# A hybrid encoder step on one Trainium2 core: the next block's activation differences move to mid-block and through DRAM, and a block's last and first steps move later

## The chip, the core and the metric

The kernel runs on one core of a Trainium2 chip. A core has five engines that each work through their own queue in order: TensorE (PE in the profile, with PEld for loading weights into it), VectorE (DVE), ScalarE (ACT), GpSimd (POOL) and SyncE (SP). SP here issues nearly all transfers between DRAM and the on-chip memory. The metric is the time of one execution in microseconds. The median of three runs of the kernel before is 2237.77 us (2236.51 to 2239.1).

## The reference, cut to what matters

The program is one layer of a streaming encoder for 2048 prompt frames and 64 further frames, 1024 features each, in float32.

```
q, k, v, u, vm = project(x @ w_in)
mix = concat(rmsnorm(window_attention(q, k, v)), rmsnorm(u * (w_s vm + b))) @ w_out
h   = layernorm(alpha * x + mix)
gu  = h @ w_gate_up                       # 1024 -> 2 * 2816
f   = (silu(gu[:, :2816]) * gu[:, 2816:]) @ w_down
y   = layernorm(alpha * h + f)
```

The change concerns the last three lines alone, the feed-forward part, which takes the second two thirds of the time.

## The kernel before

**Blocks and chunks.** The 2112 frames are cut into four blocks (512, 512, 512 and 576 frames; 17 tiles of 128 frames, the last with 64). For each block the hidden width 2816 is worked through in 22 chunks of 128 (NFF). A float32 product is made of three fast ones: each operand is split into a high part (a cast by ScalarE, L106) and a low part (a subtraction, L107, by VectorE or by POOL), and hi x hi, hi x lo and lo x hi are added in PSUM.

**Seven products for eight.** h @ w_gate_up is a two by two block product (frames in two halves by gate and up, features in two halves), and it is computed with the Strassen-Winograd scheme: seven products, numbered 1 to 7 (P1 to P7 here), for eight. For that the kernel needs sums and differences of the weights (`sums`, `form`; kept in DRAM after block 0 as wf_d and loaded from there later) and differences of the activations: with b11, b12, b21, b22 for the quarters of h (by feature half and frame half), P5 takes b12 - b11, P6 takes b22 - (b12 - b11), P7 takes b22 - b12 and P4 takes b21 - (b22 - (b12 - b11)); P1, P2 and P3 take b11, b21 and b22. Each operand lies, split, in a tile of its own (hf1 to hf7), with one buffer each: the next block's can be written only when the product of the old block's last chunk has read it.

**The order.** `order` lists the products of a block: P1, 5, 6, 2, 7 of the first chunk, then for each further chunk P1 of it, P4 and P3 of the chunk before, and P5, 6, 2, 7; at the end P4 and P3 of the last: 154 products. A product is 12 matmuls (L788 to L790) into one of three PSUM banks of its chunk (accA, accB, accC). P1, P6, P7 and P4 add up in accA, and between them ScalarE copies the bank out (`keep`, L794), before the next of them may go on writing there. `make` prepares the weights of the product five places ahead (LOOK), in one of seven buffers.

**Everything else is hung on positions of that list** (`at`, `todo`): after the product at a position, the functions registered there are issued, and each engine gets them in that order. Per two chunks these are: four loads and splits of w_down (`load_d`, `split_d`), and one down unit per tile and half (`down`: 6 matmuls, then L1129 adds the result to y). A block's last down units, with the tiles' last steps (`finish_steps`: two bn_stats, the aggregate and a pow on POOL (L86); norm, which first makes a small factor with shift_of on VectorE (L1151) and then scales on ScalarE (L1166); gain on VectorE, L1170; shift on POOL, L1174, and the store) and the load of the next block's y tile (`new_y`, L1136) fall among the first products of the next block.

**The differences before.** `prep_steps(b + 1)` loads b11 and b12 some 20 positions ahead of the boundary, subtracts on POOL (L691), loads b22 and b21 at the boundary and goes on subtracting there in a shared tile, with the splits into hf (`put`) between the subtractions.

## Time and profile before

| | us |
|---|---|
| median of three runs | 2237.77 |
| the profiled execution | 2239.35 |
| its span, first to last instruction | 2237.6 |
| TensorE busy in it | 2122.9 (95%) |
| VectorE, ScalarE, POOL busy | 1488.9, 955.5, 602.7 |
| mean granted TensorE clock | 0.974 of full speed |

In the profile a row of instructions has its start, its duration, engine, source line, operation, what it writes and reads, and in brackets how long the engine stood idle before it and what ended that. A row of the table of stretches has a stretch, its length, busy time and number of instructions of each engine, the granted share of TensorE's clock, the busy share of the DMA engines and what they moved.

### The profile page before, as it was taken

The numbers are of one execution on the slowest core, as the hardware profiler recorded it, in microseconds if no ns is written. First come the engines' busy times: TensorE is split into PE (matmuls) and PEld (weight loads), VectorE is DVE, ScalarE is ACT, GpSimd is POOL, SyncE is SP. The second block draws the span as 40 slices with busy tenths as digits, with TensorE's granted clock in tenths as the row PEclk, the third lists the DMA queues.
The fourth block names the chain that finished last, engine by engine and source line by source line (L and its number), as shares of the span: only waits on it lengthen the run. The fifth ranks groups of instructions, "written<-read, shape, count | busy, mean of one in ns | idle before, by whom it ended". The sixth has DMA issues, their size and how long they took to land.

```text
span 2237.6 us, 35543 instructions
## 1 busy us (share of the span) xinstructions
PE 2122.9 (95%) x13219; PEld 1901.1 (85%) x13219; DVE 1488.9 (67%) x2919; ACT 955.5 (43%) x2255; POOL 602.7 (27%) x542
## 2 busy tenths in 40 slices
PE   8999999989998999998799999979999979999996
PEld 6888888867886899997799999879999969999994
DVE  6877777787896788887755555764555674444446
ACT  6666666654443444444333333433333332323332
POOL 0222222231224545555311112331111331111112
PEclk9999999999999999999899999989999989999998
DMA  5111111145646767676566667666666656555551
GB/s 194 38 39 39 39 38 47 35 137 177 222 164 223 258 229 250 222 244 240 202 235 228 211 216 241 217 230 225 218 209 231 244 182 231 193 193 186 191 180 57
DMA packets 161132, 400.23 MB, mean 179 GB/s; under 512 B 19744, under 2 KB 45600, under 8 KB 160960
## 3 DMA queue, kind: packets, MB, share of 16 engines
q1 hardware_dynamic: 140432, 379.29, 49.7%
q10 hardware_dynamic: 20352, 18.35, 2.4%
q8 instruction: 104, 1.70, 0.3%
q14 instruction: 68, 0.56, 0.1%
q0 software_dynamic: 176, 0.33, 0.0%
HBM read 316.84 MB, written 81.07 MB: 178 GB/s over the span
## 4 chain that ended last, share of the span: by engine, by line
PE 47%; DVE 4%; ACT 1%; issue 1%; DVEq 0%; ACTq 0%
PE pd L152 6%; PE pd L153 6%; PE accA L788 6%; PE pd L154 6%; PE accA L790 6%; PE accA L789 6%; PE accC L788 3%; PE accC L790 3%; PE accC L789 3%; PE accB L789 1%; PE accB L790 1%; PE accB L788 1%; DVE y L1170 0%; ACT wd L106 0%; DVE hf L107 0%
## 5 line engine op out<-in xcount | busy, mean ns | idle before, releaser
L107 POOL TENSOR_TENSOR wf<-guraw,wf 128x512 fp32r<-128x512 f32 x173 | 241.1, 1394 | 821.5 <-ACT wf L106 798.1
L788 PE MATMUL accA<-hf,wf 128*128 128x256 f32 (+1 forms) x1408 | 410.5, 292 | 44.6 <-ACT a L794 39.9
L790 PE MATMUL accA<-hf,wf 128*128 128x256 f32 (+1 forms) x1408 | 407.3, 289 | 0.8 <-POOL wf L107 0.6
L789 PE MATMUL accA<-hf,wf 128*128 128x256 f32 (+1 forms) x1408 | 405.0, 288 | 0.0
L1129 DVE TENSOR_TENSOR y<-pd,y 128x512 f32<-128x512 f32 (+1 forms) x364 | 249.8, 686 | 185.2 <-PE pd L154 176.6
L788 PEld LDWEIGHTS accA<-hf,wf 128*128 128x128 f32 x1408 | 269.1, 191 | 57.6 <-ACT a L794 44.2
L152 PE MATMUL pd<-wd,ff 128*128 128x512 f32 (+1 forms) x728 | 291.1, 400 | 9.8 <-ACT wd L106 9.8
L153 PE MATMUL pd<-wd,ff 128*128 128x512 f32 (+1 forms) x728 | 289.9, 398 | 0.5 <-DVE wd L107 0.5
L154 PE MATMUL pd<-wd,ff 128*128 128x512 f32 (+1 forms) x728 | 287.6, 395 | 0.0
L789 PEld LDWEIGHTS accA<-hf,wf 128*128 128x128 f32 x1408 | 270.5, 192 | 8.5
L790 PEld LDWEIGHTS accA<-hf,wf 128*128 128x128 f32 x1408 | 269.1, 191 | 1.4 <-POOL wf L107 0.8
L107 DVE TENSOR_TENSOR wd<-draw,wd 128x512 fp32r<-128x512 f32 x176 | 171.7, 979 | 71.7 <-ACT wd L106 66.3
L794 ACT COPY a<-accA 128x256 f32<-128x256 f32 (+1 forms) x264 | 99.6, 377 | 262.6 <-PE accA L790 260.4
L788 PE MATMUL accC<-hf,wf 128*128 128x256 f32 (+1 forms) x704 | 203.6, 289 | 0.6 <-ACT wf L106 0.6
L790 PE MATMUL accC<-hf,wf 128*128 128x256 f32 (+1 forms) x704 | 202.7, 288 | 0.3 <-DVE wf L107 0.3
L789 PE MATMUL accC<-hf,wf 128*128 128x256 f32 (+1 forms) x704 | 201.6, 286 | 0.0
L106 ACT CAST ff<-a 128x256 fp32r<-128x256 f32 (+1 forms) x176 | 72.7, 413 | 289.0 <-DVE a L801 289.0
L154 PEld LDWEIGHTS pd<-wd,ff 128*128 128x128 f32 (+1 forms) x728 | 135.9, 187 | 35.1
L106 ACT CAST wf<-guraw 128x512 fp32r<-128x512 f32 x264 | 163.0, 618 | 5.5 <-PE po L154 2.9
L152 PEld LDWEIGHTS pd<-wd,ff 128*128 128x128 f32 (+1 forms) x728 | 136.5, 187 | 29.7 <-ACT wd L106 11.5
L153 PEld LDWEIGHTS pd<-wd,ff 128*128 128x128 f32 (+1 forms) x728 | 136.6, 188 | 18.3 <-DVE wd L107 2.0
L107 DVE TENSOR_TENSOR ff<-a,ff 128x256 fp32r<-128x256 f32 (+1 forms) x176 | 91.2, 518 | 84.4 <-ACT ff L106 84.4
(282 smaller groups left out, 4833.5 us busy)
## 6 DMA issues: line engine op xcount, KB each, us to landing
wf<-wf_d SPq DMA_DIRECT2D x264, 512.0 KB, 4.5
guraw<-in_w_gate_up_dram SPq DMA_DIRECT2D x110, 512.0 KB, 4.9
wf_d<-wf SPq DMA_DIRECT2D x88, 512.0 KB, 5.6
draw<-in_w_down_dram SPq DMA_DIRECT2D x176, 256.0 KB, 4.4
guraw<-in_w_gate_up_dram SPq DMA_DIRECT2D x66, 256.0 KB, 2.9
x<-in_xT_prompt_dram SPq DMA_DIRECT2D x32, 256.0 KB, 3.1
catx<-cat_d SPq DMA_DIRECT2D x16, 512.0 KB, 3.6
catx<-in_x_prompt_dram SPq DMA_DIRECT2D x16, 512.0 KB, 4.6
```

Source lines behind the costliest of these rows:

```text
L106: nc.scalar.copy(hi, src)
L107: (on or nc.vector).tensor_tensor(out=lo, in0=src, in1=hi.bitcast(F32), op=ALU.subtract)
L152: nc.tensor.matmul(out, ah, bh, start=(i == 0), stop=False)
L153: nc.tensor.matmul(out, ah, bl, start=False, stop=False)
L154: nc.tensor.matmul(out, al, bh, start=False, stop=(i == n - 1))
L788: nc.tensor.matmul(ps, wh, hh, start=(new and k == 0), stop=False, skip_group_check=not new)
L789: nc.tensor.matmul(ps, wh, hl, start=False, stop=False, skip_group_check=not new)
L790: nc.tensor.matmul(ps, wl, hh, start=False, stop=(k == 3), skip_group_check=not new)
L794: nc.scalar.copy(part[i, key][:, :n], ps)
L1129: nc.vector.tensor_tensor(out=y, in0=pd[:m], in1=y, op=ALU.add)
```

## The change

The differences of the next block are made some 100 to 64 products ahead of its first one, with loads of their own, and stored in DRAM (hs_d). Near the boundary each operand then needs one load per half (`fetch`) and its split (`put`). The last down units of a block move six positions later, the last steps of its tiles five to nine; shift_of becomes a step of its own, two positions ahead of the norm. The first down units of the next block move some three to five positions later and go by half, not by tile, and the loads and splits of w_down around are placed anew. The diff, cut to that:

```diff
+    hs_d = [{p: dram.tile([P, 4, TB[b] // 2], F32, name=f"hs_d{b}_{p}") for p in (4, 5, 6, 7)} for b in range(NB)]
...
+    def later_steps(b):
...
+        def sub(out, x, y, kk, prod):
+            if (out, kk) not in t:
+                t[out, kk] = piece("hsum")
+            nc.gpsimd.tensor_tensor(out=t[out, kk], in0=t[x, kk], in1=t[y, kk], op=ALU.subtract)
+            nc.sync.dma_start(out=hs_d[b][prod][:, 2 * kk:2 * kk + 2], in_=t[out, kk])
+
+        def fetch(prod, kk, tag):
+            t[prod, kk] = piece(tag)
+            where = {1: (0, 0), 2: (1, 0), 3: (1, 1)}.get(prod)
+            src = hs_d[b][prod][:, 2 * kk:2 * kk + 2] if where is None else (
+                h_d[b][:, 4 * where[0] + 2 * kk:4 * where[0] + 2 * kk + 2, where[1] * n:(where[1] + 1) * n])
+            nc.sync.dma_start(out=t[prod, kk], in_=src)
...
+        for kk in range(2):
+            q = -100 + 24 * kk
+            yield q, lambda kk=kk: load("b11", kk, 0, 0)
+            yield q, lambda kk=kk: load("b12", kk, 0, 1)
+            yield q + 1, lambda kk=kk: load("b22", kk, 1, 1)
+            yield q + 1, lambda kk=kk: load("b21", kk, 1, 0)
+            yield q + 6, lambda kk=kk: sub("t1", "b12", "b11", kk, 5)
+            yield q + 8, lambda kk=kk: sub("t2", "b22", "t1", kk, 6)
+            yield q + 10, lambda kk=kk: sub("b12", "b22", "b12", kk, 7)
+            yield q + 12, lambda kk=kk: sub("b21", "b21", "t2", kk, 4)
+        for prod, tag, fetch_at, put_at in ((1, "hraw", -24, -8), (5, "hraw", -22, -5), (6, "hsum", -20, -4), (2, "hraw", -6, -2),
+                                            (7, "hraw", -3, 0), (4, "hsum", -1, 2), (3, "hraw", 1, 4)):
+            for kk in range(2):
+                yield fetch_at + kk, lambda prod=prod, kk=kk, tag=tag: fetch(prod, kk, tag)
+                yield put_at + kk, lambda prod=prod, kk=kk: put(prod, kk)
...
         def norm():
-            shift_of(s_, m)
             nc.scalar.activation(y_t[t][:m], y_t[t][:m], AF.Identity, scale=s_["rs"][:m, 0:1], bias=s_["rs"][:m, 1:2])
...
-        return [lambda: stats(s_, (z(0), z(1)), m, 0), lambda: (stats(s_, (z(0), z(1)), m, 1), moments(s_, m)), norm, gain, shift]
+        return [lambda: stats(s_, (z(0), z(1)), m, 0), lambda: (stats(s_, (z(0), z(1)), m, 1), moments(s_, m)),
+                lambda: shift_of(s_, m), norm, gain, shift]
...
-            if c in (0, NFF // 2 - 1) or last and c == NFF // 2 - 2:
+            if c == 0 and b:
+                d_load, d_split = (-5, 1, -3, 2), (0, 6, 3, 7)
+            elif c == 1 and b:
+                d_load, d_split = (-8, -1, -4, 1), (-3, 7, 2, 8) if last else (-3, 5, 1, 6)
+            elif c == NFF // 2 - 1 and not last:
+                d_load, d_split = (0, 2, 1, 6), (5, 7, 6, 9)
+            elif last and c == NFF // 2 - 2:
...
-                    units_.sort(key=lambda e: e[1])
-                    where = (3, 4, 6, 7, 9, 10, 12, 13, 14, 15)
...
+                    where = (6, 10, 12, 14, 15, 16, 17, 18, 19, 20) if last else (6, 10, 12, 14, 15, 16, 17, 18)
...
-                        at(p0 + 4 + 2 * k + h, lambda b=b, c=c, t=t, h=h: down(b, c, t, h))
+                        at(p0 + 10 + 2 * k + h, lambda b=b, c=c, t=t, h=h: down(b, c, t, h))
                     steps = finish_steps(t)
-                    for q, f in zip((6, 7, 10, 11, 12), steps):
+                    for q, f in zip((11, 12, 14, 16, 17, 19), steps):
                         at(p0 + 2 * k + q, f)
-                    at(p0 + 2 * k + 14, lambda t=new.pop(0): new_y(t)) if new else None
+                    at(p0 + 2 * k + 21, lambda t=new.pop(0): new_y(t)) if new else None
         if not last:
-            for pos, f in prep_steps(b + 1):
-                at(first + NO - 1 + pos, f)
+            for pos, f in later_steps(b + 1):
+                at(first + NO + pos, f)
```

On ScalarE, at the boundary from block 1 to block 2, these were the rows up to the first copy of the new block's accA (a0<-accA); hf6 and hf7 are the split operands of P6 and P7, and hsum holds a difference that POOL makes:

```order
L106 CAST hf6_15650<-hsum_15283 128x512
L106 CAST hf7_15617<-hraw_15208 128x512
L823 ACTIVATE a1_15550<-a1_15550 128x256
L106 CAST ff_15635<-a1_15550 128x256
L106 CAST hf6_15650<-hsum_15316 128x512
L106 CAST wf_15689<-guraw_15511 128x512
L794 COPY a0_15705<-accA_15692 128x256
```

Now, up to the same copy; hf2 is the operand of P2, b21 as loaded:

```order
L877 ACTIVATE a1_15633<-a1_15633 128x256
L108 CAST ff_15714<-a1_15633 128x256
L108 CAST hf2_15726<-hraw_15646 128x512
L108 CAST wf_15764<-guraw_15599 128x512
L848 COPY a0_15780<-accA_15767 128x256
L108 CAST hf7_15784<-hraw_15697 128x512
```

The splits of differences ahead of the copy have gone, and those of P7 stand behind it.

On POOL, at the same boundary, the last steps of block 1's four tiles stood so; yrs is the pow, y the shift, wf the low part of weights:

```order
L86 TENSOR_TENSOR yrs_15866<-rs_e_15867,neg_half_201 128x1
L107 TENSOR_TENSOR wf_15880<-guraw_15740,wf_15880 128x512
L86 TENSOR_TENSOR yrs_15929<-rs_e_15930,neg_half_201 128x1
L86 TENSOR_TENSOR yrs_15997<-rs_e_15998,neg_half_201 128x1
L1174 TENSOR_TENSOR y_11929<-y_11929,ln2b_7948 128x512 x2
L107 TENSOR_TENSOR wf_16040<-guraw_15740,wf_16040 128x512
L86 TENSOR_TENSOR yrs_16063<-rs_e_16064,neg_half_201 128x1
L1174 TENSOR_TENSOR y_12256<-y_12256,ln2b_7948 128x512 x2
L107 TENSOR_TENSOR wf_16095<-guraw_15943,wf_16095 128x512
L1174 TENSOR_TENSOR y_12304<-y_12304,ln2b_7948 128x512 x2
```

Now:

```order
L88 TENSOR_TENSOR yrs_16042<-rs_e_16043,neg_half_217 128x1
L109 TENSOR_TENSOR wf_16056<-guraw_15813,wf_16056 128x512
L88 TENSOR_TENSOR yrs_16106<-rs_e_16107,neg_half_217 128x1
L109 TENSOR_TENSOR wf_16118<-guraw_15967,wf_16118 128x512
L88 TENSOR_TENSOR yrs_16172<-rs_e_16173,neg_half_217 128x1
L88 TENSOR_TENSOR yrs_16242<-rs_e_16243,neg_half_217 128x1
L1227 TENSOR_TENSOR y_11964<-y_11964,ln2b_7964 128x512 x2
L109 TENSOR_TENSOR wf_16271<-guraw_15967,wf_16271 128x512
L1227 TENSOR_TENSOR y_12442<-y_12442,ln2b_7964 128x512 x2
L109 TENSOR_TENSOR wf_16329<-guraw_16188,wf_16329 128x512
L1227 TENSOR_TENSOR y_12502<-y_12502,ln2b_7964 128x512 x2
```

All four pow operations stand ahead of the first shift now; the fourth stood behind it and behind a weight form.

On SP, at the same boundary, the issues from the weights of P7 of the new block's first chunk (wf_d0_7) to those of P5 of its second (wf_d1_5) were (guraw is w_gate_up, y the next tile):

```order
L754 DMA wf_15657<-wf_d0_7_111 128x1024
L686 DMA hraw_15686<-h_d2_89 128x2x256
L754 DMA wf_15738<-wf_d0_3_108 128x1024
L735 DMA guraw_15740<-in_w_gate_up_dram 128x1024
L735 DMA guraw_15742<-in_w_gate_up_dram 128x512
L1136 DMA y_15758<-hy_d8_99 128x1024
L754 DMA wf_15762<-wf_d1_5_113 128x1024
```

Now, from the second row after the weights of P7 on (draw is w_down):

```order
L741 DMA hsum_15762<-hs_d2_4_116 128x512
L1166 DMA draw_15782<-in_w_down_dram 128x512
L741 DMA hsum_15787<-hs_d2_4_116 128x512
L1166 DMA draw_15805<-in_w_down_dram 128x512
L741 DMA hraw_15809<-h_d2_89 128x2x256
L808 DMA wf_15811<-wf_d0_3_124 128x1024
L789 DMA guraw_15813<-in_w_gate_up_dram 128x1024
L789 DMA guraw_15815<-in_w_gate_up_dram 128x512
L1190 DMA y_15831<-hy_d8_99 128x1024
L741 DMA hraw_15836<-h_d2_89 128x2x256
L808 DMA wf_15838<-wf_d1_5_129 128x1024
```

The loads of the differences for P4 (hsum) and of h for P3 (hraw) and two of w_down have come between; the last hraw is the fifth issue counted from the weights of P3.

## Rows read from the trace of the kernel before

**Rows 1.** The page, busy time of each engine (share of the span, instructions).

```profile
PE 2122.9 (95%) x13219; PEld 1901.1 (85%) x13219; DVE 1488.9 (67%) x2919; ACT 955.5 (43%) x2255; POOL 602.7 (27%) x542
```

**Rows 2.** TensorE: a product, a down unit, first P6 matmul of two blocks.

```profile
1014.36 0.28 PE L788 MATMUL accA<-hf,wf 128*128 128x256 f32 x1
...
1015.80 0.40 PE L152 MATMUL pd<-wd,ff 128*128 128x512 f32 x1
...
1017.20 0.28 PE L788 MATMUL accC<-hf,wf 128*128 128x256 f32 x1
...
1059.54 0.58 PE L788 MATMUL accA<-hf,wf 128*128 128x256 f32 x1 [6.96 <-ACT a L794]
...
1425.11 0.39 PE L788 MATMUL accA<-hf,wf 128*128 128x256 f32 x1 [0.74 <-ACT a L794]
```

**Rows 3.** Stretches: PE, PEld, DVE, ACT, POOL busy (count), clock, DMA, GB/s.

```profile
1000.00:1020.00 20.00, 20.00 (x141) 18.64 (x140) 15.82 (x23) 8.26 (x18) 11.88 (x10) 1.00 0.85 303
1040.00:1060.00 20.00, 12.31 (x82) 11.09 (x81) 11.62 (x19) 7.41 (x17) 10.80 (x8) 0.86 0.77 264
1060.00:1080.00 20.00, 18.80 (x103) 16.95 (x103) 14.63 (x23) 7.45 (x17) 5.58 (x5) 0.79 0.48 160
1100.00:1120.00 20.00, 9.33 (x46) 7.87 (x47) 11.76 (x17) 7.82 (x14) 9.77 (x7) 0.66 0.61 230
1420.00:1440.00 20.00, 16.84 (x101) 14.86 (x101) 15.59 (x24) 8.75 (x19) 5.90 (x4) 0.91 0.62 216
1460.00:1480.00 20.00, 8.80 (x50) 7.16 (x50) 14.88 (x22) 6.59 (x12) 10.09 (x8) 0.69 0.60 203
1780.00:1800.00 20.00, 15.70 (x94) 14.28 (x93) 17.06 (x22) 10.64 (x22) 10.64 (x7) 0.91 0.57 189
1820.00:1840.00 20.00, 14.43 (x95) 12.75 (x93) 15.21 (x26) 7.51 (x13) 10.27 (x9) 0.91 0.51 183
1840.00:1860.00 20.00, 14.87 (x82) 13.88 (x83) 10.92 (x18) 6.67 (x13) 7.88 (x6) 0.75 0.78 266
```

**Rows 4.** Waits of TensorE, 700 to 2200 us: total, times, longest.

```profile
PE accA L788 <- ACT a L794: 39.9, 13, 8.0
```

**Rows 5.** Instructions of POOL and ScalarE at boundary 0/1.

```profile
1047.68 1.29 POOL L691 TENSOR_TENSOR hsum<-hraw,hsum 128x512 f32<-128x512 f32 x1 [6.07 <-DMA hraw<-h_d]
...
1058.09 0.61 ACT L106 CAST hf<-hsum 128x512 fp32r<-128x512 f32 x1
```

**Rows 6.** Instructions of ScalarE and VectorE in the second place of boundary 0/1.

```profile
1101.12 1.24 ACT L1166 ACTIVATE y<-y,yrs 128x1024 f32<-128x1024 f32 x1 [2.62 <-DVE yrs L1151]
...
1108.78 1.21 DVE L1151 SCALAR_TENSOR_TENSOR yrs<-ymv,yrs 128x1 f32<-128x1 f32 x1
...
1110.03 1.24 ACT L1166 ACTIVATE y<-y,yrs 128x1024 f32<-128x1024 f32 x1 [3.98 <-DVE yrs L1151]
```

**Rows 7.** Gains on VectorE; POOL beside the second; a shift on POOL.

```profile
1087.66 1.28 DVE L1170 TENSOR_TENSOR y<-y,ln2g 128x512 f32<-128x512 f32 x2
...
1094.31 2.38 DVE L1170 TENSOR_TENSOR y<-y,ln2g 128x512 f32<-128x512 f32 x2
...
1094.32 1.83 POOL L107 TENSOR_TENSOR wf<-guraw,wf 128x512 fp32r<-128x512 f32 x1 [1.20 <-issue]
...
1106.67 3.31 POOL L1174 TENSOR_TENSOR y<-y,ln2b 128x512 f32<-128x512 f32 x2 [1.86 <-DVE y L1170]
```

**Rows 8.** A stretch; issues (count, size, us to landing); one issue on SP.

```profile
1480.00:1490.00 10.00, 10.00 (x64) 9.16 (x64) 4.05 (x9) 3.44 (x9) 4.51 (x4) 0.94 0.98 368
...
wf<-wf_d SPq DMA_DIRECT2D x264, 512.0 KB, 4.5
...
hraw<-h_d SPq DMA_DIRECT2D x24, 256.0 KB, 5.1
...
1410.26 0.41 SPq L754 DMA_DIRECT2D wf<-wf_d  x1
```

**Rows 9.** A subtraction on POOL in block 0.

```profile
1014.61 1.30 POOL L691 TENSOR_TENSOR hsum<-hraw 128x512 f32<-128x512 f32 x1
```

More of the change, by code (lines that the diff above doesn't have):

```diff
@@ L710, in prep_steps, with piece, load, put @@
                 yield at_ + kk, lambda fn=fn, a=a: fn(*a)
+    def later_steps(b):
+        t = {}
+        n = TB[b] // 2
+        def piece(tag):
+            return f1.tile([P, 2 * NHX], F32, name=tag, tag=tag, bufs={"hraw": 4, "hsum": 2}[tag])[:, :2 * n].rearrange(
+                "p (k t) -> p k t", k=2)
+        def load(key, kk, kh, sh):
+            t[key, kk] = piece("hraw")
+            k0 = 4 * kh + 2 * kk
+            nc.sync.dma_start(out=t[key, kk], in_=h_d[b][:, k0:k0 + 2, sh * n:(sh + 1) * n])
+        def sub(out, x, y, kk, prod):
[9 more added lines that the diff above has]
+            nc.sync.dma_start(out=t[prod, kk], in_=src)
+        def put(prod, kk):
+            if kk == 0:
+                forms[b, prod] = f1.tile([P, 8 * NHX], F32R, name=f"hf{prod}", tag=f"hf{prod}", bufs=1)[:, :8 * n].rearrange(
+                    "p (s k t) -> p s k t", s=2, k=4)
+            o = forms[b, prod][:, :, 2 * kk:2 * kk + 2]
+            split(o[:, 0], o[:, 1], t.pop((prod, kk)))
+        for kk in range(2):
[13 more added lines that the diff above has]
+                yield put_at + kk, lambda prod=prod, kk=kk: put(prod, kk)
@@ L1283, in hybrid_step @@
                 where = (2, 3, 4, 5, 7, 8, 9, 10, 12, 13) if last else (2, 4, 5, 7, 9, 10, 12, 13)
-                units_ = [(h, t) for h in range(2) for t in TILES[b]]
                 if c == 0 and b:
-                    units_.sort(key=lambda e: e[1])
-                    where = (3, 4, 6, 7, 9, 10, 12, 13, 14, 15)
-                for k, (h, t) in enumerate(units_):
+                    where = (6, 10, 12, 14, 15, 16, 17, 18, 19, 20) if last else (6, 10, 12, 14, 15, 16, 17, 18)
+                elif c == 1 and last:
+                    where = (3, 4, 5, 6, 7, 9, 10, 11, 12, 13)
+                for k, (h, t) in enumerate((h, t) for h in range(2) for t in TILES[b]):
                     at(p0 + where[k], lambda b=b, c=c, t=t, h=h: down(b, c, t, h))
```

## The prediction

> **What bounds the kernel now.** I read the engines' busy times first. TensorE is busy for 95% of the span [rows 1], so only time in which it stands still or runs at half clock can be won. Its own work in the second half is fixed: 12 matmuls of a product take 1.44 us (1014.36 to 1015.80), the 6 of a down unit 1.40 us [rows 2]. A block of 22 chunks has 154 products and 88 down units, so 154 x 1.44 + 88 x 1.40 = 345.0 us of work. The same matmul (first of the product P6 of a block's first chunk) starts at 1059.54 in block 1 and at 1425.11 in block 2 [rows 2]: 365.6 us. So about 20.6 us per block are lost, and the question is where.
>
> The table of stretches answers it [rows 3]. In mid-block TensorE is busy 20.00 of 20.00 us at full clock. Around a boundary it isn't. I count a stretch's loss as its idle time plus (1 - granted clock) x its busy time:
> - Boundary 0/1: 7.69 + 1.72, 1.20 + 3.95, and later 10.67 + 3.17: 28.4 us.
> - Boundary 1/2: 3.16 + 1.52, later 11.20 + 2.73: 18.6 us (the block period said 20.6).
> - Boundary 2/3: 4.30 + 1.41, later 5.57 + 1.30 and 5.13 + 3.72: 21.4 us.
>
> The sum is 68.4 us, in two places: 25.0 us when the new block begins and 43.4 us some 35 to 45 us later. In the second place idle time is 32.6 and the clock 10.9, so each idle microsecond drags about a third of one behind it; in the first the two are 16.4 and 8.6.
>
> The list of waits then says for what TensorE waits: almost only for ScalarE's copy of a PSUM bank, accA (L794), 39.9 us in 13 waits [rows 4]. ScalarE is far from full, so something stands before the copy in its queue.
> - First place: a split of the differences does. It waits for POOL's subtractions, and the first of four in a row starts only when h_d data have landed, at 1047.68; ScalarE splits the last hsum at 1058.09, then comes the copy, and TensorE starts at 1059.54 [rows 5, 2].
> - Second place: the norm (L1166) of a finished tile. It starts at 1101.12 after 2.62 us of waiting and at 1110.03 after 3.98, each time for the tiny shift_of (L1151) on VectorE, which took 1.21 us instead of its usual fraction at 1108.78 [rows 6]. Two norms are 8.91 us apart: ScalarE and VectorE wait for each other in turn, and the copy and the splits of w_down are queued behind.
>
> **The change part by part.** Slots are counted from a block's first product (slot 0).
>
> Differences in mid-block. Per boundary 8 subtractions of 1.29 us (10.3 us of POOL) leave the boundary. Instead of 8 transfers there are 30: 8 loads and 8 stores in mid-block, 14 loads at the boundary, all issued by SP; SP waits at each store for POOL, and behind it stand weight loads that have five products of lead. In block 0, where POOL is busiest, two of the subtractions of before ran from 1014.61 on [rows 9], and TensorE was busy 20.00 of 20.00 with POOL at 11.88 and VectorE at 15.82 [rows 3]. Four within 7 products and 4 units (15.7 us) make POOL 9.3 + 5.2 = 14.5 of 15.7: it still fits. Bounds: 0, and 10.3 if none is covered, in block 0 alone. I take 1 us, near the row.
>
> First steps. The 14 splits of 0.61 us on ScalarE [rows 5] stay as many; none waits for POOL any longer, and in the new order the copy that TensorE needs has one split and one weight cast ahead of it. What is late next is the last load, the second half of h for P3. It is the fifth issue from a weight load that needs the buffer of product 0; at 0.41 us an issue [rows 8] it goes out 2.1 us after slot 1 begins. It lands 5.1 us later [rows 8] and takes some 1.3 us to split, 0.61 on ScalarE [rows 5] and as much on VectorE: 8.5 us. P3's second half is needed after six products and a half, 9.4 us. That is in time with 0.9 us of room. Taken away entirely, the first place costs 0; if it stays as in the two later boundaries, 4.7 or 5.7. I take 3 per boundary, half of it and a little; for the first boundary too, since its extra 9 us came from the subtractions' late start.
>
> Last steps. The down units of the last chunk pair move from slots 3 to 10 to slots 9 to 16, so slots 0 to 8 are products alone. The four steps of a tile become five, and shift_of stands two slots ahead of the norm instead of in front of it. On POOL all four small pow operations now stand ahead of the first shift, where one stood behind two tensor operations. So a norm finds its scale ready, the turn-taking loses its cause, and new_y, a load that waits for the output's store, is still two slots later. The cover gets thinner though: the gains fall on slots 16 to 22, of which five have no down unit. A gain took 1.28 us alone and 2.38 with a POOL operation beside it [rows 7]. Three of the four will meet POOL's shifts (3.31 us at 1106.67 [rows 7]): 3 x 1.10 = 3.3 us, with a third for the clock 4.4; I take 5. Bounds: 1 (all covered) and the 13.8 to 15.7 of now.
>
> On this POOL and VectorE stretch each other in the rows. The Trainium skill (SBUF — State Buffer, Who interferes with whom) goes further: a VectorE instruction with two inputs in SBUF and a GpSimd instruction that reads SBUF hold the shared port for a whole instruction, and the other blocks. The trace agrees with a lengthening of 1.10 for a pair of gains, but not of one whole POOL operation for each.
>
> The new times of the w_down loads and splits, the order of the units by half, and block 0's first chunk pair, which now has the ordinary offsets, I cost at nothing: each split still stands slots ahead of its unit, beside products.
>
> Sum: 3 x 3 + 3 x 5 + 1 = 25 us stay of 68.4: 43.4 us are won. The profiled execution took 2239.35 us (span 2237.6), so 2196.0; the median of the three runs is 1.6 lower, hence **2194 us**.
>
> **The rivals.**
> - Nearly all goes: 2 us stay per boundary. For it: nothing in mid-block loses anything. Against: slots 0 to 8 have no cover. 2237.8 - 62.4 = 2175 us.
> - Transfers. SP's 23 issues from the load for slot -1 to that for slot 9 carry 8.65 MB (7 x 512, 2 x 768, 3 x 256, 8 x 256, 512 KB), where before 19 carried 7.60 MB. TensorE has 11 x 1.44 + 4 x 1.40 = 21.4 us for them: 404 GB/s, above the 368 of the best stretch [rows 8]. At 368 they end 2 us late, which the weights' lead hides (six products, 8.6 us, less 4.5 to land: 4.1). At the 266 of 1840 to 1860 [rows 3] they take 32.5 us: 11.1 late, 7.0 idle, 9.3 with the clock. That is 6.3 more than taken, three times: 2213 us.
> - Every gain operation waits out a POOL operation: 8 x 1.29 = 10.3, with the clock 13.7 instead of 5 per boundary: 2220 us. For it: the 2.38; against: the 1.28 of its neighbour. It is what the rule of the Trainium skill named above would give.
> - Slower: the turn-taking stays, through the gains and the mults that still alternate between ScalarE and VectorE. Four tiles at 8.91 us are 35.6 us, now in slots 15 to 24, where TensorE has 20.0 us of work: 15.6 idle, 20.8 with the clock, and 3 for the first place: 71.4 + 1, that is 2242 us. It decides from 8.7 us a tile on. Against it: its link, the norm behind shift_of, is the one that is cut.
> - The change doesn't do what it says: the norm then waits for statistics instead and the splits for the loads: 2235 us.
>
> **How the numbers follow.** Forecast (2184 to 2206) 0.43; nearly all 0.18; transfers 0.11; port 0.10; slower 0.11; no effect 0.05; something between 0.02. A measurement of this kernel can tell 0.2%, some 4.5 us. Faster: 0.43 + 0.18 + 0.11 + 0.10 + 0.02 = 0.84; same 0.05; slower 0.11. The range reaches from the case in which nearly all goes to just above the port's: 2175 to 2228.
>
> **What would show it.** Right: the same matmul in blocks 1 and 2 about 353 us apart (345 + 8); waits of accA for L794's successor under 12 us in place of 39.9; norms under 6 us apart; no POOL subtraction within 40 us of a boundary and no idle TensorE beside those in mid-block. Transfers: waits of TensorE for weights or for hf in slots 2 to 9. Port: gains of 2.4 us and more, four times per boundary. Wrong altogether: norms still 9 us apart, or half clock for over 10 us after a boundary.

## The result, and the profile after

The kernel after takes 2204.64 us (median of four runs, 2202.89 to 2205.52) against 2238.43 of the kernel before in the same runs: a ratio of 0.9849 [0.9832, 0.9867]. 33.8 us were won where 43.4 were forecast; 2204.64 lies inside the range. The profiled execution took 2202.89 us with a span of 2201.1.

In the kernel after, the matmuls of a product are L842 to L844, the copy of accA is L848, the splits are L108 (ScalarE) and L109, a down unit's matmuls L154 to L156 and its add L1183, shift_of L1205, norm L1219, gain L1223, shift L1227, the loads of the operands L741. First the page's line of busy times, and the first P6 matmul of a first chunk in blocks 1 and 2:

```profile
PE 2113.0 (96%) x13219; PEld 1895.4 (86%) x13219; DVE 1483.8 (67%) x2919; ACT 955.9 (43%) x2255; POOL 612.0 (28%) x542
```

```profile
1048.82 0.28 PE L842 MATMUL accA<-hf,wf 128*128 128x256 f32 x1
...
1405.40 0.28 PE L842 MATMUL accA<-hf,wf 128*128 128x256 f32 x1
```

The instruction counts are those of [rows 1]: the work has not changed. TensorE is busy 9.9 us less; its mean granted clock is 0.984, before 0.974. The two matmuls are 356.6 us apart, where they were 365.6 [rows 2] and 353 were forecast. The table of stretches (columns as in [rows 3]) shows what is left:

```profile
900.00:920.00 20.00, 20.00 (x135) 18.37 (x134) 17.50 (x24) 9.17 (x21) 15.26 (x11) 1.00 0.86 302
...
1040.00:1060.00 20.00, 18.06 (x135) 17.12 (x136) 14.17 (x25) 11.65 (x26) 4.43 (x3) 1.00 1.03 402
...
1060.00:1080.00 20.00, 20.00 (x134) 18.36 (x133) 13.58 (x29) 7.25 (x17) 4.91 (x5) 1.00 0.66 227
...
1080.00:1100.00 20.00, 18.55 (x131) 16.96 (x130) 18.36 (x28) 7.42 (x13) 12.17 (x10) 1.00 0.66 218
1100.00:1120.00 20.00, 15.13 (x92) 14.29 (x93) 12.05 (x23) 8.32 (x18) 6.68 (x5) 0.83 0.95 337
1400.00:1420.00 20.00, 17.44 (x125) 16.77 (x125) 13.78 (x23) 10.96 (x24) 4.36 (x3) 0.91 0.84 294
1440.00:1460.00 20.00, 17.44 (x127) 16.09 (x125) 18.29 (x28) 6.36 (x13) 13.28 (x10) 1.00 0.62 206
1460.00:1480.00 20.00, 16.23 (x97) 15.16 (x98) 11.05 (x21) 8.60 (x18) 5.62 (x5) 0.83 0.99 359
1760.00:1780.00 20.00, 19.26 (x136) 18.55 (x135) 14.68 (x25) 13.13 (x27) 4.43 (x3) 1.00 0.87 311
1800.00:1820.00 20.00, 16.28 (x111) 15.14 (x109) 16.79 (x24) 7.77 (x14) 12.91 (x10) 0.98 0.65 201
1820.00:1840.00 20.00, 18.56 (x106) 17.27 (x107) 10.65 (x19) 6.96 (x16) 5.42 (x4) 0.85 0.98 367
```

Counted as in the prediction, the first place now costs 1.9, 4.1 and 0.7 us, and the second 8.9, 9.1 and 8.3. The first row lies in block 0, where the subtractions now are: POOL is busy for 15.26 of 20 us, and TensorE loses nothing. In the second place VectorE is busy for 18.4 and 18.3 of the 20 us ahead of the longest wait (16.5 between 1080 and 1100 us before). In the 20 us with the wait it is busy for 12.05, about as before (11.76 [rows 3]). The list of TensorE's waits, 700 to 2200 us:

```profile
PE accA L842 <- ACT a L848: 22.7, 11, 5.8
...
PE accC L842 <- ACT hf L108: 3.6, 2, 2.2
```

The wait for the copy fell from 39.9 [rows 4] to 22.7. The second line is new. It is the first place: P3 (in accC) waits for the second half of its operand. Of boundary 0/1 these are the first matmul of P5 (slot 1), the two issues of w_gate_up on SP, the load's issue, the split on ScalarE that waited for it, and TensorE:

```profile
1047.38 0.28 PE L842 MATMUL accC<-hf,wf 128*128 128x256 f32 x1
...
1048.73 2.11 SPq L789 DMA_DIRECT2D guraw<-in_w_gate_up_dram  x2
...
1051.37 0.42 SPq L741 DMA_DIRECT2D hraw<-h_d  x1
...
1057.65 0.62 ACT L108 CAST hf<-hraw 128x512 fp32r<-128x512 f32 x1 [1.59 <-DMA hraw<-h_d]
...
1058.32 0.38 PE L842 MATMUL accC<-hf,wf 128*128 128x256 f32 x1 [1.43 <-ACT hf L108]
...
1415.70 0.38 PE L842 MATMUL accC<-hf,wf 128*128 128x256 f32 x1 [2.21 <-ACT hf L108]
```

The load went out 4.0 us after slot 1 began, and the split could start 6.28 us after the issue. The five issues didn't follow each other at 0.41 us: SP waited 2.1 us before the two loads of w_gate_up, and 2.0 at boundary 1/2, for a low part of weights on VectorE; there too the load went out 4.0 us after slot 1 began. The last row is the same matmul at boundary 1/2. Now the second place of boundary 0/1, the instructions of VectorE, POOL, ScalarE and TensorE in order of time:

```profile
1083.62 1.28 DVE L1223 TENSOR_TENSOR y<-y,ln2g 128x512 f32<-128x512 f32 x2
...
1086.34 0.15 DVE L1205 SCALAR_TENSOR_TENSOR yrs<-ymv,yrs 128x1 f32<-128x1 f32 x1
...
1088.19 2.99 POOL L1227 TENSOR_TENSOR y<-y,ln2b 128x512 f32<-128x512 f32 x2
...
1088.55 1.46 DVE L109 TENSOR_TENSOR wd<-draw,wd 128x512 fp32r<-128x512 f32 x1 [1.02 <-ACT wd L108]
...
1090.27 3.15 DVE L1223 TENSOR_TENSOR y<-y,ln2g 128x512 f32<-128x512 f32 x2
...
1091.13 1.74 POOL L109 TENSOR_TENSOR wf<-guraw,wf 128x512 fp32r<-128x512 f32 x1
1092.83 3.00 POOL L1227 TENSOR_TENSOR y<-y,ln2b 128x512 f32<-128x512 f32 x2
...
1093.34 1.25 DVE L1205 SCALAR_TENSOR_TENSOR yrs<-ymv,yrs 128x1 f32<-128x1 f32 x1
...
1095.39 0.72 DVE L109 TENSOR_TENSOR ff<-a,ff 128x256 fp32r<-128x256 f32 x1 [0.47 <-ACT ff L108]
1096.04 2.38 DVE L1223 TENSOR_TENSOR y<-y,ln2g 128x512 f32<-128x512 f32 x2
...
1097.83 3.40 POOL L1227 TENSOR_TENSOR y<-y,ln2b 128x512 f32<-128x512 f32 x2
...
1098.34 1.76 DVE L109 TENSOR_TENSOR wd<-draw,wd 128x512 fp32r<-128x512 f32 x1
1100.02 0.68 DVE L1183 TENSOR_TENSOR y<-pd,y 128x512 f32<-128x512 f32 x1
...
1102.28 1.24 ACT L1219 ACTIVATE y<-y,yrs 128x1024 f32<-128x1024 f32 x1
...
1104.06 0.69 DVE L109 TENSOR_TENSOR wd<-draw,wd 128x512 fp32r<-128x512 f32 x1 [1.22 <-ACT wd L108]
...
1104.45 0.36 ACT L848 COPY a<-accA 128x256 f32<-128x256 f32 x1
...
1104.87 0.58 PE L842 MATMUL accA<-hf,wf 128*128 128x256 f32 x1 [5.79 <-ACT a L848]
```

Read the first number after the start. A pair of gains takes 1.28 us alone, and 3.15 and 2.38 where POOL is at work, on shifts or on low parts of weights (1091.13); a low part of w_down 0.69, and 1.46 and 1.76; the tiny shift_of 0.15, and 1.25; a low part of ff 0.43 elsewhere, and 0.72. The excess is 1.87 + 1.10 + 0.77 + 1.07 + 1.10 + 0.29 = 6.2 us, against a wait of TensorE of 5.79. The add of a down unit, one of whose inputs lies in PSUM, keeps its 0.68 at 1100.02 although a shift runs beside it. And the norm (1102.28) waits for nothing any more: the link on which the prediction laid the stall has gone, and one long wait per boundary is still there (5.79, 5.79 and 5.16 us).

### The profile page after: what moved, and what is told of

Its sections match the earlier page's. It is cut to its first block, busy times and chain, and to the rows that moved or that the text cites. A ratio compares the mean times of both kernels' runs of the same rounds, so it can differ in the third digit from the quotient of the medians.

```text
span 2201.1 us, 35670 instructions
## 1 busy us (share of the span) xinstructions
PE 2113.0 (96%) x13219; PEld 1895.4 (86%) x13219; DVE 1483.8 (67%) x2919; ACT 955.9 (43%) x2255; POOL 612.0 (28%) x542
## 4 chain that ended last, share of the span: by engine, by line
PE 74%; DVE 16%; ACT 4%; issue 3%; DMA 2%; POOL 1%; SPq 0%; DVEq 0%; ACTq 0%; POOLq 0%
PE accA L842 7%; PE pd L154 7%; PE pd L155 7%; PE pd L156 7%; PE accA L844 7%; PE accA L843 7%; PE accC L843 4%; PE accC L842 4%; PE accC L844 4%; PE pj L154 2%; PE pj L155 2%; PE pj L156 2%; PE po L154 2%; PE po L155 2%; PE po L156 2%
## 5 line engine op out<-in xcount | busy, mean ns | idle before, releaser
L109 POOL TENSOR_TENSOR wf<-guraw,wf 128x512 fp32r<-128x512 f32 x173 | 243.6, 1408 | 792.4 <-ACT wf L108 790.3
L842 PE MATMUL accA<-hf,wf 128*128 128x256 f32 (+1 forms) x1408 | 410.9, 292 | 26.6 <-ACT a L848 22.7
L844 PE MATMUL accA<-hf,wf 128*128 128x256 f32 (+1 forms) x1408 | 407.6, 289 | 0.2 <-DVE wf L109 0.2
L1183 DVE TENSOR_TENSOR y<-pd,y 128x512 f32<-128x512 f32 (+1 forms) x364 | 250.0, 687 | 184.2 <-PE pd L156 179.0
L842 PEld LDWEIGHTS accA<-hf,wf 128*128 128x128 f32 x1408 | 270.0, 192 | 38.2 <-ACT a L848 25.8
L154 PE MATMUL pd<-wd,ff 128*128 128x512 f32 (+1 forms) x728 | 287.8, 395 | 1.4 <-ACT wd L108 1.4
L156 PE MATMUL pd<-wd,ff 128*128 128x512 f32 (+1 forms) x728 | 286.2, 393 | 0.0
L844 PEld LDWEIGHTS accA<-hf,wf 128*128 128x128 f32 x1408 | 269.7, 192 | 0.9 <-DVE wf L109 0.9
L109 DVE TENSOR_TENSOR wd<-draw,wd 128x512 fp32r<-128x512 f32 x176 | 172.3, 980 | 61.4 <-ACT wd L108 56.1
L848 ACT COPY a<-accA 128x256 f32<-128x256 f32 (+1 forms) x264 | 99.8, 378 | 253.3 <-PE accA L844 250.9
L842 PE MATMUL accC<-hf,wf 128*128 128x256 f32 (+1 forms) x704 | 203.1, 289 | 4.3 <-ACT hf L108 3.6
L844 PE MATMUL accC<-hf,wf 128*128 128x256 f32 (+1 forms) x704 | 202.5, 288 | 0.6 <-DVE wf L109 0.6
L108 ACT CAST ff<-a 128x256 fp32r<-128x256 f32 (+1 forms) x176 | 72.7, 413 | 288.8 <-DVE a L855 284.2
L108 ACT CAST wf<-guraw 128x512 fp32r<-128x512 f32 x264 | 163.2, 618 | 4.8 <-PE po L156 2.9
L156 PEld LDWEIGHTS pd<-wd,ff 128*128 128x128 f32 (+1 forms) x728 | 134.6, 185 | 34.6
L154 PEld LDWEIGHTS pd<-wd,ff 128*128 128x128 f32 (+1 forms) x728 | 134.9, 185 | 20.4 <-ACT wd L108 1.9
L155 PEld LDWEIGHTS pd<-wd,ff 128*128 128x128 f32 (+1 forms) x728 | 135.0, 185 | 17.2 <-DVE wd L109 0.5
L109 DVE TENSOR_TENSOR ff<-a,ff 128x256 fp32r<-128x256 f32 (+1 forms) x176 | 88.7, 504 | 84.6 <-ACT ff L108 84.6
```

What stands on the lines that cost most here:

```text
L108: nc.scalar.copy(hi, src)
L109: (on or nc.vector).tensor_tensor(out=lo, in0=src, in1=hi.bitcast(F32), op=ALU.subtract)
L154: nc.tensor.matmul(out, ah, bh, start=(i == 0), stop=False)
L155: nc.tensor.matmul(out, ah, bl, start=False, stop=False)
L156: nc.tensor.matmul(out, al, bh, start=False, stop=(i == n - 1))
L842: nc.tensor.matmul(ps, wh, hh, start=(new and k == 0), stop=False, skip_group_check=not new)
```

## The experiments

Twelve kernels were run, each against the kernel before on the same chip. For all of them I count the loss more finely than by stretches: the distance of the starts of two matmuls that follow each other, less the usual distance for their kind, summed over the first and the second place (us, boundary 0/1 + 1/2 + 2/3). Idle time and half clock are both in it. The places come from one profiled execution of each kernel. The interval of a ratio is some 0.0015 to either side, so two kernels less than about 5 us apart are told apart by their places more than by their times.

| kernel | median us | ratio to before | first place | second place |
|---|---|---|---|---|
| before | 2238.43 | 1 | 12.0 + 5.5 + 5.7 = 23.2 | 14.2 + 14.1 + 13.9 = 42.2 |
| after | 2204.64 | 0.9849 [0.9832, 0.9867] | 2.3 + 4.6 + 1.0 = 7.9 | 8.9 + 8.6 + 7.5 = 25.0 |
| 1 steps only | 2209.40 | 0.9875 [0.9860, 0.9889] | 14.1 | 25.6 |
| 2 differences only | 2214.54 | 0.9898 [0.9883, 0.9913] | 0.8 | 43.9 |
| 3 late first units | 2214.82 | 0.9897 [0.9879, 0.9915] | 0.0 | 44.5 |
| 4 old spacing | 2210.24 | 0.9876 [0.9863, 0.9890] | 9.6 | 29.1 |
| 5 joined | 2205.05 | 0.9853 [0.9839, 0.9868] | 7.5 | 25.7 |
| 6 old splits | 2211.29 | 0.9876 [0.9858, 0.9894] | 7.5 | 33.4 |
| 7 no shift | 2190.85 | 0.9790 [0.9775, 0.9804] | 6.8 | 14.3 |
| 8 one input | 2196.15 | 0.9810 [0.9794, 0.9826] | 6.7 | 19.0 |
| 9 fused | 2200.34 | 0.9837 [0.9821, 0.9852] | 7.7 | 21.1 |
| 10 fetch early | 2200.65 | 0.9831 [0.9815, 0.9847] | 4.5 | 24.9 |
| 11 both | 2195.45 | 0.9809 [0.9794, 0.9823] | 4.0 | 19.3 |
| 12 both, earlier | 2201.68 | 0.9838 [0.9825, 0.9852] | 5.2 | 26.6 |

### What each half of the change does

**1. Steps only.** The positions of after, the differences of before.

```diff
-            for pos, f in later_steps(b + 1):
-                at(first + NO + pos, f)
+            for pos, f in prep_steps(b + 1):
+                at(first + NO - 1 + pos, f)
```

> The new order of last and first steps alone; the differences are made as before (loads, subtractions and splits at the boundary). Theory (the two parts mend two separate places): the first place loses its old 25.0 us again instead of 7.9, the second keeps the 25 us of the changed kernel: 2204.6 + 17 = 2222 us, second place as in the changed kernel (one wait of 5.3 to 5.8 us per boundary). Rival (the parts need each other: slots 0 to 8 without down units leave the late subtractions no cover): the first place loses more than 35 us, 2232 us or more.

Both missed: 2209.4. TensorE's two long waits at boundary 0/1 in this kernel:

```profile
1055.13 0.58 PE L842 MATMUL accA<-hf,wf 128*128 128x256 f32 x1 [5.92 <-ACT a L848]
...
1111.36 0.58 PE L842 MATMUL accA<-hf,wf 128*128 128x256 f32 x1 [5.80 <-ACT a L848]
```

The second place is as in after. But the first place, which I had ascribed to the differences, fell by 9 us though they still stand at the boundary: taking the down units and their adds and splits out of slots 3 to 8 seems to give the splits room, which is a reading of the rows and not a test.

**2. Differences only.** The differences of after; units, steps and w_down as before.

```diff
-            for pos, f in prep_steps(b + 1):
-                at(first + NO - 1 + pos, f)
+            for pos, f in later_steps(b + 1):
+                at(first + NO + pos, f)
```

> The differences in mid-block and through DRAM alone; last and first steps stand as in the kernel before. Theory (two separate places): the first place falls from 25.0 to about 8 us, the second keeps 43.5: 2238.4 - 17 = 2221 us, two waits of 3 and 8 us per boundary in the second place. Rival (the late splits of ScalarE now run into the down units and steps that stand early): no gain in the first place, 2232 us or more.

2214.54: further down than the theory had it, and the rival is out. TensorE's waits:

```profile
PE accA L839 <- ACT a L845: 31.0, 10, 8.1
PE pd L153 <- ACT wd L107: 10.0, 4, 3.5
```

The second place is untouched. The first is mended nearly whole (0.8), better than in after: here the old block's down units still lie beside the loads. In this kernel P3's last load goes out 5.6 us after slot 1 begins, later than in after; but P3 begins 15.0 us after slot 1 instead of 8.6, and nothing waits. So the halves don't add. Alone they win 28.4 and 23.3 us, together 33.8: in the first place each mends much of the same loss, and with the units gone P3's load has no cover.

### What mended half of the second place

**3. Late first units.** After, with the old block's last units, steps and w_down at the positions of before; only the new block's first units and their splits stay late.

```diff
-            elif c == NFF // 2 - 1 and not last:
-                d_load, d_split = (0, 2, 1, 6), (5, 7, 6, 9)
-            elif last and c == NFF // 2 - 2:
+            elif c == NFF // 2 - 1 and not last or last and c == NFF // 2 - 2:
...
-                        at(p0 + 10 + 2 * k + h, ...
+                        at(p0 + 4 + 2 * k + h, ...
-                    for q, f in zip((11, 12, 14, 16, 17, 19), steps):
+                    for q, f in zip((6, 7, 10, 10, 11, 12), steps):
...
-                    at(p0 + 2 * k + 21, ...
+                    at(p0 + 2 * k + 14, ...
```

> After, but a block's last down units, its tiles' last steps, new_y and the last w_down loads and splits stand at their positions of before again (units from slot 3, steps at the old distances, shift_of still with the norm's neighbours); the new block's first units and their w_down splits stay late, and the differences stay in mid-block. Theory (the later and by-half place of the new block's first units, with their w_down splits, is what mends the second place): first place about 2 as with the differences alone, second place 20 to 28 instead of 25, waits of TensorE there 4 to 7 per boundary, 2196 to 2205 us. Rival (the later last steps mend it): second place 36 to 44, waits of 10 to 12 per boundary as with the differences alone, 2211 to 2216 us.

2214.82: the rival. The rows of ScalarE and TensorE show the turn-taking of [rows 6] again:

```profile
1083.16 1.24 ACT L1219 ACTIVATE y<-y,yrs 128x1024 f32<-128x1024 f32 x1 [2.66 <-DVE yrs L1205]
...
1092.12 1.24 ACT L1219 ACTIVATE y<-y,yrs 128x1024 f32<-128x1024 f32 x1 [4.06 <-DVE yrs L1205]
1093.26 0.35 ACT L848 COPY a<-accA 128x256 f32<-128x256 f32 x1
...
1093.67 0.58 PE L842 MATMUL accA<-hf,wf 128*128 128x256 f32 x1 [10.71 <-ACT a L848]
```

Norms 8.96 us apart, the copy behind the norm, TensorE behind the copy. The new block's first units win nothing by themselves; what counts is the later place of the old block's last units and steps, with the loads and splits of w_down that belong to them.

**4. Old spacing.** After, with each last step at the distance from its unit that it had before.

```diff
-                    for q, f in zip((11, 12, 14, 16, 17, 19), steps):
+                    for q, f in zip((12, 13, 16, 16, 17, 18), steps):
...
-                    at(p0 + 2 * k + 21, ...
+                    at(p0 + 2 * k + 20, ...
```

> The changed kernel with the last steps at the old distances from the down units (statistics 2 and 3 positions after the first unit, norm with shift_of 6, gain 7, shift and store 8, next load 10, for now 1, 2, 4, 6, 7, 9, 11); the units and the next block's first steps stay late. The fourth pow stands behind the first shift again. Theory (the spacing mends the second place: pow ahead of the shifts and room between the steps): the second place goes back towards 40 us, 2215 us or more. Rival (what mends it is the place of the down units and w_down splits around: TensorE's waits on them are gone whatever the steps' spacing): 2202 to 2208 us.

2210.24, between the two: with the place alone the second place goes from 44 to 29, the wider spacing (and with it the order of the pow operations) brings the last 4.

**5. Joined.** After, with shift_of back in front of the norm, in the same step; all else stays.

```diff
         def norm():
+            shift_of(s_, m)
...
-                lambda: shift_of(s_, m), norm, gain, shift]
+                lambda: None, norm, gain, shift]
```

> The changed kernel with shift_of back in front of the norm (the step of its own two positions ahead is undone; all positions stay). Theory (turn-taking of ScalarE and VectorE through shift_of was the cause of half the old loss in the second place): the norms wait for shift_of again, the second place goes from 25 towards 40 us, 2215 us or more. Rival (the later positions and the pow operations ahead of the shifts suffice; the separate step does nothing): 2203 to 2207 us.

2205.05: the rival. ScalarE's waits in this kernel:

```profile
ACT y L1220 <- DVE yrs L1205: 22.5, 9, 5.0
```

The norms wait 22.5 us again, up to 5.0 at a time (before 23.9, up to 4.0), and the time is that of after. So the link that the prediction called the cause isn't worth anything where the steps now stand. What it is worth where they stood before was not tested: no run cuts the link alone there.

**6. Old splits.** After, with w_down of the new block's first chunk pair loaded and split at the offsets of before.

```diff
             if c == 0 and b:
-                d_load, d_split = (-5, 1, -3, 2), (0, 6, 3, 7)
+                d_load, d_split = (-8, -1, -5, -3), (-3, 1, -1, 1)
```

> After, but the loads and splits of w_down of a new block's first chunk pair stand at their offsets of before (loads -8, -1, -5, -3, splits -3, 1, -1, 1 instead of -5, 1, -3, 2 and 0, 6, 3, 7). TensorE's order is that of after. Theory (those splits, low parts on VectorE in the stretch of the gains, weigh in the second place): moved ahead of the first units they pile up with the gains, the wait of 5.96 grows to 8 or more, 2209 to 2214 us. Rival (their place doesn't matter, the place of the units does): waits 5 to 7, 2202 to 2207 us.

2211.29. The theory's time came (2209 to 2214), its wait didn't. TensorE's list:

```profile
PE accA L842 <- ACT a L848: 24.4, 15, 3.7
```

The one long wait of 5.2 to 5.8 us became three waits of 1.0 to 3.7 per boundary, and the second place went from 25 to 33: the place of these loads and splits, which I had costed at nothing, is worth 6.7 us. Only 3.6 us of the 8.4 are more idle time (21.4 for 17.8 us); the rest is work at the lower clock (granted 0.87 between 1080 and 1120 us, for 0.91 in after).

### What is left in the second place

**7. No shift.** POOL's addition of ln2_b is left out in 12 tiles.

```diff
-            for h in range(2):
-                nc.gpsimd.tensor_tensor(out=z(h)[:m], in0=z(h)[:m], in1=ln2b[...], op=ALU.add)
```

> The changed kernel without POOL's addition of ln2_b in the blocks' last steps (left out of the result of 12 tiles); all else in its order. Theory (VectorE's operations and POOL's shifts hold each other up; the excess over the undisturbed durations between 1083 and 1106 us is 6.2 us, the wait 5.8): the second place falls from 25 to 5 us or less, 2185 us, and a pair of gains takes 1.3 us throughout. Rival (turn-taking of ScalarE and VectorE in the order of their queues): the norms and the wait stay, 2200 to 2205 us. Rival (the chain of store and next load on SP): the stores leave some 3 us earlier, gain of at most 3 us per boundary, but gains still stretched.

2190.85, 13.8 us less than after, which is not what the theory said: the second place kept 14.3 us, not 5 or less, and a pair of gains is still stretched. Nor is it a rival's: the last one has the stretched gains, but at most 3 us per boundary, and 4.6 came. TensorE's waits, then VectorE and POOL:

```profile
PE accA L842 <- ACT a L848: 10.3, 11, 1.8
PE accA L842 <- DMA wf<-wf_d: 4.8, 3, 2.2
```

```profile
1092.81 1.29 POOL L109 TENSOR_TENSOR wf<-guraw,wf 128x512 fp32r<-128x512 f32 x1 [1.22 <-issue]
...
1092.87 2.39 DVE L1223 TENSOR_TENSOR y<-y,ln2g 128x512 f32<-128x512 f32 x2
...
1097.27 1.64 POOL L109 TENSOR_TENSOR wf<-guraw,wf 128x512 fp32r<-128x512 f32 x1 [3.17 <-ACT wf L108]
...
1097.68 1.78 DVE L109 TENSOR_TENSOR wd<-draw,wd 128x512 fp32r<-128x512 f32 x1
```

What POOL does here are low parts of weights, not shifts, and they hold VectorE up just the same. The low part of w_down at 1097.68 ends at 1099.46, 0.55 us after the POOL operation beside it (1098.91); alone it takes 0.69. So it waits until POOL's operation ends. Of the 6.2 us of excess 1.11 + 1.09 = 2.2 stay; that is 4.0 less, and the longest wait fell by as much, from 5.79 to 1.80. The second line of waits is new: TensorE, now earlier, waits 4.8 us for weights from DRAM, so part of the 14.3 us is another limit that after didn't reach.

**8. One input.** A gain becomes an instruction of the same length that reads one tile.

```diff
-                nc.vector.tensor_tensor(out=z(h)[:m], in0=z(h)[:m], in1=ln2g[...], op=ALU.mult)
+                nc.vector.bn_stats(s_["st"][:m, h], z(h)[:m])
```

> The changed kernel with each of the 24 gain operations in the blocks' last steps replaced by a statistics operation on the same half tile (the product with ln2_g is left out of 12 tiles): the same nominal 0.68 us of VectorE in the same place, but one input. Theory (what holds VectorE up is a second input from SBUF beside POOL): the gains' share of the excess goes, 1.87 + 1.10 us per boundary, and POOL's shifts return from 3.0 to 2.6 us: 2 to 4 us per boundary, 2193 to 2199 us; shift_of and the splits of w_down stay stretched. Rival (VectorE is simply full there): no change, 2203 to 2206 us.

2196.15, as the theory has it. VectorE and POOL in this kernel:

```profile
1095.02 2.73 POOL L1227 TENSOR_TENSOR y<-y,ln2b 128x512 f32<-128x512 f32 x2
1096.51 1.27 DVE L1223 BATCH_NORM_STATS2 yst<-y 128x6 f32<-128x512 f32 x2
...
1105.24 2.54 POOL L1227 TENSOR_TENSOR y<-y,ln2b 128x512 f32<-128x512 f32 x2 [3.03 <-DVE yst L1223]
```

With one input in SBUF the pair at 1096.51 keeps its 1.27 us beside a shift that runs until 1097.75, and the four pairs of shifts take 2.5 to 3.0 us in place of 2.8 to 3.4. The work on POOL is the same. So it is not POOL's presence but the second input that costs. A gain also writes a whole half tile where these statistics write six columns; that this isn't the reason is seen in after, where the add of a down unit writes as much, has one input in SBUF and takes 0.68 to 0.69 us each time, beside POOL or not. The Trainium skill (SBUF — State Buffer, Who interferes with whom) says this: outside the 2-port modes of VectorE, an instruction of VectorE contends with a GpSimd one that reads SBUF if it has two inputs there, not if it has one. The rows agree. Here too TensorE waits for weights from DRAM (5.1 us in 3 waits), so the 19.0 us that stay are not all the old wait.

### Using it

**9. Fused.** Norm, gain and shift of a half become two instructions of VectorE, none on POOL or ScalarE.

```diff
+        def both(h):
+            hs = slice(h * 512, (h + 1) * 512)
+            nc.vector.scalar_tensor_tensor(out=z(h)[:m], in0=z(h)[:m], scalar=s_["mv"][:m, 0:1], in1=ln2g[:m, hs],
+                                           op0=ALU.subtract, op1=ALU.mult)
+            nc.vector.scalar_tensor_tensor(out=z(h)[:m], in0=z(h)[:m], scalar=s_["rs"][:m, 0:1], in1=ln2b[:m, hs],
+                                           op0=ALU.mult, op1=ALU.add)
...
-                lambda: shift_of(s_, m), norm, gain, shift]
+                lambda: None, lambda: both(0), lambda: both(1), store]
```

> The changed kernel with a tile's last steps as two operations per half on VectorE (subtract mean and times ln2_g; times rstd and plus ln2_b); no norm on ScalarE, no shift on POOL. VectorE gets 4 x 1.28 = 5.1 us more per boundary than undisturbed gains, but in the changed kernel its excess beside POOL was 6.2 us. Theory (the stretch is what costs): the second place falls, not as far as without shifts at all (2191 us): 2193 to 2199 us. Rival (VectorE's load in the slots without down units is what costs): no gain or a loss, 2204 us or more.

2200.34, 4.3 us less than after and just short of the theory: the longest wait for the copy fell from 5.8 to 3.8 us, not further. VectorE now does the work of norm and shift as well; that this is what it pays back was not tested apart.

**10. Fetch early.** P3's loads one position earlier.

```diff
-    ... (7, "hraw", -3, 0), (4, "hsum", -1, 2), (3, "hraw", 1, 4)):
+    ... (7, "hraw", -3, 0), (4, "hsum", -1, 2), (3, "hraw", 0, 4)):
```

> The changed kernel with the two loads of h for P3 one position earlier (0 and 1 for 1 and 2), so that the second goes out before the weights of P3, the two loads of w_gate_up and the y tile instead of behind them. Theory (the first place's 7.9 us are the wait of P3 for that load, 2.1 us of issues late): the first place falls to 3 us or less, 2199 to 2201 us. Rival (the transfers are at their limit there, 402 GB/s between 1040 and 1060 us, so another load is late in its place): no change, 2203 to 2206 us.

2200.65: the time is a hit; the first place fell to 4.5 us, not to 3 or less. The stretch of boundary 1/2, for the 17.44 and 0.91 of after:

```profile
1400.00:1420.00 20.00, 19.09 (x146) 18.35 (x145) 14.91 (x26) 12.59 (x28) 4.38 (x3) 1.00 0.89 327
```

The wait for the load was the first place there. At 0/1 2.3 us remain, 1.05 of them a wait for VectorE's low part of the same operand.

**11. Both** (9 and 10 together).

> Both of the last two edits: the fused steps on VectorE and the earlier loads for P3. Theory (two separate places): their gains add, 2188 to 2194 us. Rival (what one place wins the other loses): not faster than the better of the two alone.

2195.45, 9.2 less than after where the two alone gave 4.3 and 4.0; the forecast of 2188 to 2194 was a little too low. It beats both kernels.

**12. Both, with the last steps earlier.**

```diff
-                    for q, f in zip((11, 12, 14, 16, 17, 19), steps):
+                    for q, f in zip((11, 12, 13, 14, 15, 16), steps):
...
-                    at(p0 + 2 * k + 21, ...
+                    at(p0 + 2 * k + 18, ...
```

> The kernel with both edits (fused steps on VectorE, earlier loads for P3) with the fused steps two positions earlier, the store and the next y tile's load three. Theory (VectorE's work in the slots without down units is what is left in the second place, 15 us): part of it moves under the down units of slots 9 to 16, 2188 to 2193 us. Rival (VectorE is as full under the down units): no change or a loss, 2195 us or more.

2201.68, the rival: 6 us are lost again. Steps nearer to the units meet more of VectorE's other work there, which is a reading, not shown.

## Why the prediction was right or wrong, point by point

- **What bounds the kernel:** right. Nearly all that was won lies in the two places; 23.2 + 42.2 became 7.9 + 25.0, a gain of 32.5 of the 33.8.
- **Differences in mid-block, 1 us:** nothing is lost there (first row of the stretches), in the block with the busiest POOL.
- **First steps, 3 per boundary:** 2.3, 4.6 and 1.0, 7.9 for 9. The load named as late next is the one. Its 0.9 us of room was more than used up: it went out 4.0 us after slot 1 began and not 2.1, because SP waited some 2 us before the loads of w_gate_up, and its split could start after 6.28 us, not 5.1. What the step missed besides is that the moved units alone bring 9.1 of this place's 15.3 us (run 1), and that they take the cover from P3's load (run 2).
- **Last steps, 5 per boundary:** this is the term that was mis-sized: 8.3. The gains did what was forecast, 1.87 + 1.10 = 3.0 for 3.3, though two pairs were longer and not three. Left out were the other instructions of VectorE with two inputs in SBUF, two low parts of w_down, shift_of and a low part of ff, 3.2 us more, and POOL's low parts of weights, which hold VectorE up as its shifts do. Run 7 takes 4.0 of the 6.2 us of excess away and 4.0 of the wait with them; the second place falls by 10.7 of 25.0, by 6.0 in run 8. Of the 14.3 us that stay in run 7 some 5 are the wait for weights; the rest, VectorE's work beside POOL's low parts and the lower clock, was not taken apart.
- **"The turn-taking loses its cause":** it ended, but not by the cut that I named. With the link restored (run 5) the time stays; with the link and the old positions (run 3) the turn-taking is back. The place of the old block's last units and steps takes the second place from 44 to 29 (runs 3 and 4), the spacing to 25, and in it the place of the splits of w_down, costed at nothing, weighs 8 (run 6). Why the later place helps in detail, whether by the units, the splits of the last pair or new_y, was not taken apart further. By the diff the last steps stand four to seven positions later, not five to nine, the new block's first units three to seven, and a tile's steps are five before and six now.
- **The sum:** 43.4 forecast, 33.8 measured; 25 us were to stay and 32.9 did (10 more in the second place, 1.1 less in the first, 1 less in mid-block). The rest is the count: 68.4 by stretches are 65.4 by starts, and 1.3 us were won outside the two places. That the time still lies in the forecast's 2184 to 2206 is in part luck: with the splits of run 6 at their old offsets, which the prediction would have priced the same, it is 2211.
- **The rivals:** "Transfers" put the limit at 368 GB/s, the best stretch near a boundary; the stretch around P3's load moved 402, and before had moved 416 between 720 and 730 us. No wait for a load of weights from DRAM is in the list of after. Of its sign, waits for hf in slots 2 to 9, 3.6 us came, at P3, and run 10 takes them away by the order of issue; with the second place shorter (runs 7 and 8) waits for weights do come. "Every gain operation waits out a POOL operation" had the price of a meeting nearly right and their number wrong: at each boundary three gain operations of eight meet one, and each of the three ends 0.55 us after it, 0.77 to 1.10 us longer than alone. That makes 3.0 of 10.3 us for the gains. The reading "not of one whole POOL operation for each" is wrong for those that meet one. "The turn-taking stays" (2242) did not come: no norm in the new positions waits for shift_of.
- **The signs:** the matmuls were 356.6 us apart for 353, and no subtraction came near a boundary. The waits for the copy did not fall under 12 us (22.7), and the norms are not under 6 us apart (6.7, 2.7 and 12.8 at boundary 0/1), though none waits for shift_of.

## What to carry to other kernels

Where an engine that runs ahead waits in a ring with another, a wait in the list needn't be what costs: give the link back alone and see (run 5). When VectorE and POOL are both in a tight stretch, count every VectorE instruction with two inputs in SBUF that starts beside a POOL operation, the smallest ones too, and charge each with the rest of that operation, whichever it is. And two edits that each mend a place share its loss: the filler work that one of them takes away may be the cover that the other needs.

## What the runs showed of the hardware that was not expected

- Between 1040 and 1060 us the DMA engines moved 402 GB/s at a busy share of 1.03, where the best 20 us before were 368 (720 to 740); a load of 256 KB then took 6.28 us until its reader could start, against a median to landing of 5.1 before [rows 8] and 5.9 in after.
- An instruction on one element per partition, shift_of, took 1.25 us in place of 0.15 beside a POOL operation. In the trace of after, between 700 and 2150 us, all 70 low parts of w_down that start while POOL is in the middle of a tile operation end 0.55 to 0.56 us after it, all nine gains that do so 0.55 to 0.56, and the three shift_of 0.01 to 0.02: the delay is what is left of POOL's operation, not a matter of size.
- With the wait of 5.79 us, which ended at 1104.87, TensorE's granted clock was 0.83 between 1100 and 1120 us, which are partly at 1.2 instead of 2.4 GHz: 2.6 us of loss behind 4.9 us of idle time in that stretch. After the wait of 1.43 us at 1058.32 it stayed at 1.00 (1060 to 1080); in the stretch with the wait of 2.21 us at 1415.70 it was 0.91.
